# Feed-forward block of a recurrent decoder step: the RMS factor moved from the operands to the products, and the openings and closings of its parts reordered

## The chip, the cores and the metric

The kernel is one program on one core of a Trainium2 chip. Its metric is the device time of one execution, in microseconds (us). TensorE is written PE (PEld is its weight load), VectorE DVE, ScalarE ACT, GpSimd POOL, and SP issues the transfers.

## What is computed

Two layers of a hybrid decoder run on 576 tokens (512 of a prompt, 8 x 8 of samples), with activations kept as eight tiles `x[k]` of 128 channels x 576 tokens. Each layer is a recurrent mixer, a SwiGLU feed-forward and a gated per-layer embedding (ple). The change touches the feed-forward alone:

```
def _rmsnorm(x, g):
    y = xf * lax.rsqrt(jnp.mean(xf * xf, axis=-1, keepdims=True) + EPS)
    return (y * g.astype(F32)).astype(x.dtype)

def _swiglu(x, w1, w3, w2):
    return (jax.nn.silu(x @ w1) * (x @ w3)) @ w2

x = x + _swiglu(_rmsnorm(x, W['g_ffn'][i]), W['ffn_w1'][i], W['ffn_w3'][i], W['ffn_w2'][i])
```

The model width is 1024 and the hidden width 2816. The factor rsqrt(mean(x^2)+eps) is one number for each token, called `r` in the kernel.

## The kernel before

Every fp32 operand is split in a high and a low part (`whi`/`wlo` for weights, `bh`/`bl` for activations, `hh`/`hl` for hidden channels): ACT copies the high part to a rounded type, DVE subtracts it from the source. A product is then three matmuls, high x high, high x low, low x high. Weight tiles come by `wraw` (SP, two raw buffers) and are split by `wsplit`. Split weights live in two buffers of the pool `wp`, whatever they are for, so a new weight can be split only when PE is done with the one before the last.

`ffn` multiplies the 2x2 blocks of (w1, w3) with the 2x2 blocks of x (upper channels `x[0..3]` and lower `x[4..7]`, first and second half of the 576 tokens) by a seven-product scheme of the Strassen-Winograd kind. Its operands: `b11` and `b1` need the upper channels alone, `b21`, `b2`, `b3`, `b4`, `b22` the lower ones too. The eleven pairs of hidden tiles are run in three parts (`PARTS`: 4, 4 and 3 pairs). A pair is seven products of 24 matmuls, in this order: `head` (w13[p,0] by b11, into `mmx`), w13[p,1] by b21 (`mmy`), u by b2 (added on `mmx`), a22 by b1 (`mmz`), a21 by b3 (on `mmx`), the `head` of the next pair, w13[p,3] by b4 (on `mmx`), u by b22 (on `mmz`). Between them `mmx` is copied to SBUF by `copied` (line 1125) and the products are added up by `block`. After each part eight `gemm`s by w2 (line 210) are added to x by `add_out` (line 361). In the last pair of a part there is no head of a next pair between the third product on `mmx` and the fourth.

At the start of `ffn` the squares of `x[k]` are summed, `rnorm` makes `r` (PE sums over channels, DVE makes the inverse root in twelve small steps, PE broadcasts, ACT copies), and then DVE makes `g * x * r` (line 1092) and the differences (lines 1097 to 1103), which `operand` splits.

The program's text gives priorities. The order on each engine is fixed when the kernel is built, by a planner with its own estimates of durations: it takes the earliest instruction in the text that it believes ready, so a later one can go ahead of one that waits. The engines then run in that order. In layer 0 the embedding's products (`ple_up`) stand between the mixer and `ffn`; in layer 1 they are done inside the mixer, and the mixer's output projection, whose results POOL adds to x (line 359), comes right before.

Of the kernel before, what the change touches and what calls it, by code (L numbers as in the profile page):

```python
# [12 lines left out]
F = mybir.dt.float32  # L13
# [3 lines left out]
AF = mybir.ActivationFunctionType  # L17
# [31 lines left out]
OUT_V = ()  # L49
# [31 lines left out]
def trunk(ctx, tc, a, stop=None):  # L81
# [21 lines left out]
    def pcol(name, i=0, n=1):  # L103
        return par[:, PAR[name] + i:PAR[name] + i + n]
# [78 lines left out]
    def wload(ap, kt, eng=V):  # L183
        return wsplit(wraw(ap, kt), kt, wp, 2, eng=eng)
# [73 lines left out]
    def half(s):  # L258
        return slice(s * HF, (s + 1) * HF)
# [84 lines left out]
    def square_add(acc, src, first, eng=V):  # L344
        if first:
            S.activation(acc, src, AF.Square)
        else:
            sq = tmp("t2", 2)[:, :src.shape[-1]]
            one = S.activation(sq, src, AF.Square)
            two = eng.tensor_tensor(acc, acc, sq, op=OP.add)  # L350
            return one.ins, two.ins

    def add_out(m, ps, r=None):
        for s in range(2):
            xh, src = x[m][:, half(s)], ps[:, s]
            if r is not None:
                t = tmp("t1", 2)[:, :HF]
                V.tensor_tensor(t, src, r[:, half(s)], op=OP.mult)
                (V if m in OUT_V else G).tensor_tensor(xh, xh, t, op=OP.add)  # L359
            else:  # L360
                V.tensor_tensor(xh, src, xh, op=OP.add)  # L361

# [696 lines left out]
    def ffn(i, ha):  # L1059
        w13, w2 = a["w13"][i], a["w2"][i]  # L1060
        with tc.tile_pool(name=f"ffn{i}", bufs=1) as hp:
# [27 lines left out]
            (xg0, t0), (xg1, t1) = ([t_.bitcast(F) for t_ in hq()] for _ in range(2))  # L1089
            for xg, k0 in ((xg0, 0), (xg1, 4)):  # L1090
                for j in range(4):
                    V.scalar_tensor_tensor(xg[:, j], x[k0 + j], pcol("g_ffn", i * KD + k0 + j), r, op0=OP.mult, op1=OP.mult)  # L1092
                if k0 == 0:
                    b11 = operand(0, xg0[:, :, :HF])
            b21 = operand(1, xg1[:, :, :HF])
            d3, d2, d1, d4 = t0[:, :, :HF], t0[:, :, HF:], t1[:, :, :HF], t1[:, :, HF:]
            V.tensor_tensor(d3, xg1[:, :, HF:], xg0[:, :, HF:], op=OP.subtract)
            V.tensor_tensor(d2, d3, xg0[:, :, :HF], op=OP.add)
            b2 = operand(2, d2, -1.0)
            V.tensor_tensor(d1, xg0[:, :, :HF], xg0[:, :, HF:], op=OP.subtract)  # L1100
            b1 = operand(3, d1)
            b3 = operand(4, d3)
            V.tensor_tensor(d4, d2, xg1[:, :, :HF], op=OP.subtract)
            b4 = operand(5, d4)
            b22 = operand(6, xg1[:, :, HF:])

            def wsum(tag, src=None):
                t = hp.tile([P, 1024], F, tag=tag, name=tag, bufs=1)
                if src is not None:
                    nc.sync.dma_start(t, src)  # L1110
                return t
# [18 lines left out]
                prod([ps[:, n, :HF] for n in range(2)], wload(w13[p, 0], KD), b11, True)  # L1130
                return ps, copied(ps, "t1")

            def block(s, outs, dst, sign):
                for n in range(2):
                    V.tensor_tensor(s[:, n], s[:, n], outs[n], op=OP.add)
                S.activation(s[:, 0], s[:, 0], AF.Silu, scale=sign)
                if sign > 0:
                    V.tensor_tensor(dst, s[:, 0], s[:, 1], op=OP.mult)
                else:
                    V.scalar_tensor_tensor(dst, s[:, 1], sign, s[:, 0], op0=OP.mult, op1=OP.mult)  # L1140

            for p0, p1 in PARTS:
                hs = []
                for p in range(p0, p1):
# [6 lines left out]
                    ys = [bank("mmy")[:, :HF] for _ in range(2)]  # L1151
                    prod(ys, wload(w13[p, 1], KD), b21, True)
                    f1, f2 = tmp("rb", 2), tmp("t2", 2)
                    block(s1, ys, f1[:, :HF], 1.0)
                    a21, a22, a11, a12 = (wsum(f"a{n}", w13[p, n]) for n in (2, 3, 0, 1))
                    u = wsum("u")
                    V.tensor_tensor(a22, a22, a21, op=OP.add)
# [3 lines left out]
                    zs = [bank("mmz", "o")[:, :HF] for _ in range(2)]  # L1161
                    prod(zs, wsplit(a22, KD, wp, 2), b1, True)
# [3 lines left out]
                    block(s3, zs, f2[:, HF:], -1.0)  # L1166
# [8 lines left out]
                    block(s2, zs, f1[:, HF:], 1.0)  # L1175
# [283 lines left out]
```

## Time and profile before

| | us |
|---|---|
| median of three runs | 1871.07 (1869.39 to 1874.81) |
| the profiled execution | 1873.93 |
| its span in the trace | 1872.2 |

The trace is of the one profiled execution; 1.7 us of it lie outside the span. Times in rows count from the span's start. A matmul's duration in a row is modelled and overlaps the next, so PE is read by counts and starts: how many matmuls a stretch holds, and what they would need at the spacing of an undisturbed stretch.

### The profile page before, as it was taken

Reading aid. Unit: us, or ns where it says so; the run is one execution under the profiler, and the core shown is the slowest. Engines: PE = TensorE matmul, PEld = TensorE weight load, DVE = VectorE, ACT = ScalarE, POOL = GpSimd, SP = SyncE. Lnnn points to the kernel's source line nnn. Section 1 sums busy time; section 2 is a strip of 40 time slices with the busy share of each in tenths; the row PEclk is TensorE's granted clock in tenths of the full one; section 3 lists DMA queues with packets and bytes.
Section 4 is the critical chain, followed back from the end, with each engine's and each line's share of the span. In section 5 each row is a group of like instructions: output and inputs, shape, how many; then the busy total and the mean of one; then the engine's idle time right before and its main releaser. Section 6 shows DMA issues by size and latency. Waiting matters only on the chain. (4 is left out here: it accounts for less than half of the span.)

```text
span 1872.2 us, 32247 instructions
## 1 busy us (share of the span) xinstructions
PE 1748.0 (93%) x13134; PEld 1693.6 (90%) x13134; DVE 1343.1 (72%) x2256; ACT 811.7 (43%) x1341; POOL 415.1 (22%) x393
## 2 busy tenths in 40 slices
PE   7899989899999999989998999998959999999994
PEld 7789979899999999989987999998959999999994
DVE  6877784886377375588996897988587637737556
ACT  6654442554254143444553444535444325415332
POOL 2433343000000000033445537455510000000002
PEclk9999999899999999989998999999979999999997
DMA  5111113244244242312231322223315424424221
GB/s 191 57 62 66 68 49 130 83 160 139 91 162 154 87 147 71 118 41 72 103 111 68 109 104 85 96 100 108 118 52 167 133 86 168 147 91 144 71 80 51
DMA packets 63124, 193.74 MB, mean 103 GB/s; under 512 B 7040, under 2 KB 12800, under 8 KB 62976
## 3 DMA queue, kind: packets, MB, share of 16 engines
q1 hardware_dynamic: 62400, 191.10, 29.8%
q8 instruction: 103, 1.69, 0.4%
q10 hardware_dynamic: 576, 0.59, 0.1%
q14 instruction: 45, 0.37, 0.1%
HBM read 177.10 MB, written 14.56 MB: 102 GB/s over the span
## 5 line engine op out<-in xcount | busy, mean ns | idle before, releaser
L174 ACT ACTIVATE whi<-wraw 128x1024 fp32r<-128x1024 f32 (+2 forms) x213 | 221.5, 1040 | 392.6 <-PE mm L210 175.3
L175 DVE TENSOR_TENSOR wlo<-wraw,whi 128x1024 fp32r<-128x1024 f32 (+1 forms) x187 | 230.4, 1232 | 73.8 <-ACT whi L174 73.0
L1220 POOL TENSOR_TENSOR ev<-ev,rb 128x288 f32<-128x288 f32 x18 | 18.1, 1034 | 952.7 <-ACT rb L255 952.7
L1120 PE MATMUL mmx<-bh,whi 128*128 128x288 f32 x704 | 211.9, 301 | 14.8 <-ACT t L1125 9.3
L1120 PE MATMUL mmx<-bh,wlo 128*128 128x288 f32 x704 | 210.6, 299 | 4.8 <-DVE wlo L175 4.7
L1120 PE MATMUL mmx<-bl,whi 128*128 128x288 f32 x704 | 210.6, 299 | 2.9 <-DVE bl L163 2.9
L193 PE MATMUL mm<-xah,whi 128*128 128x288 f32 x632 | 191.4, 303 | 3.7 <-DVE hz L264 1.7
L193 PE MATMUL mm<-xal,whi 128*128 128x288 f32 x632 | 190.2, 301 | 0.0
L193 PE MATMUL mm<-xah,wlo 128*128 128x288 f32 x632 | 189.4, 300 | 0.0
L361 DVE TENSOR_TENSOR x<-mm,x 128x288 f32<-128x288 f32 x128 | 52.4, 451 | 169.1 <-PE mm L210 159.1
L193 PE MATMUL mm<-xch,whi 128*128 128x288 f32 x536 | 161.4, 301 | 2.9 <-DVE x L361 2.9
L193 PE MATMUL mm<-xch,wlo 128*128 128x288 f32 x536 | 160.8, 300 | 0.0
L193 PE MATMUL mm<-xcl,whi 128*128 128x288 f32 x536 | 160.7, 300 | 0.0
L210 PE MATMUL mm<-hl,whi 128*128 128x288 f32 x704 | 152.0, 296 | 0.0
L210 PE MATMUL mm<-hh,whi 128*128 128x288 f32 x704 | 151.7, 296 | 0.0
L210 PE MATMUL mm<-hh,wlo 128*128 128x288 f32 x704 | 151.3, 296 | 0.0
L1120 PEld LDWEIGHTS mmx<-bh,whi 128*128 128x128 f32 x704 | 134.5, 191 | 16.9 <-ACT t L1125 10.7
L1120 PEld LDWEIGHTS mmx<-bh,wlo 128*128 128x128 f32 x704 | 135.2, 192 | 6.6 <-DVE wlo L175 6.5
L1120 PEld LDWEIGHTS mmx<-bl,whi 128*128 128x128 f32 x704 | 134.9, 192 | 3.1 <-DVE bl L163 3.1
L193 PEld LDWEIGHTS mm<-xah,whi 128*128 128x128 f32 x632 | 120.0, 190 | 7.8 <-ACT lt L497 2.1
L193 PEld LDWEIGHTS mm<-xal,whi 128*128 128x128 f32 x632 | 120.2, 190 | 2.4 <-issue 1.8
L193 PEld LDWEIGHTS mm<-xah,wlo 128*128 128x128 f32 x632 | 120.1, 190 | 1.6 <-issue 0.9
(495 smaller groups left out, 4927.4 us busy)
## 6 DMA issues: line engine op xcount, KB each, us to landing
wraw<-w SPq DMA_DIRECT2D x98, 512.0 KB, 3.4
a<-w SPq DMA_DIRECT2D x88, 512.0 KB, 3.3
wraw<-w_sin SPq DMA_DIRECT2D x40, 512.0 KB, 3.3
wraw<-w_ein SPq DMA_DIRECT2D x22, 512.0 KB, 3.3
wraw<-wg SPq DMA_DIRECT2D x16, 512.0 KB, 3.2
s<-ss SPq DMA_DIRECT2D x16, 512.0 KB, 3.5
sss<-s SPq DMA_DIRECT2D x16, 512.0 KB, 2.8
wraw<-w_sout SPq DMA_DIRECT2D x16, 512.0 KB, 3.6
```

What stands on the lines that cost most here:

```text
L174: S.activation(hi, raw, AF.Copy)
L175: eng.tensor_tensor(lo, raw, hi.bitcast(F), op=OP.subtract)
L193: PE.matmul(ps, w[:, cols], v, start=(k == 0 and i == 0), stop=(k == n - 1 and i == 2))
L210: PE.matmul(ps[:, s, :HF], w[:, j * P:(j + 1) * P], m[:, half(s)], start=(k == 0 and i == 0), stop=(k == n - 1 and i == 2))
L361: V.tensor_tensor(xh, src, xh, op=OP.add)
L1120: PE.matmul(outs[n], w[:, o], v, start=(first and k == 0 and t_ == 0), stop=(k == 3 and t_ == 2), skip_group_check=not first)
L1220: eng.tensor_tensor(v, v, r[:, half(s)], op=OP.mult)
```

## The change

The operands become `g * x`, without `r`. `r` is multiplied into the first factor of each product of the hidden layer before its silu (one more DVE multiplication in `block` and one for the fourth product), and into the results of w2 in `add_out`, whose addition goes to DVE. The sums of squares and `rnorm` are moved behind the first operands. For the first pair, its head, the head of the second pair and its a22 product, all on the upper channels, stand ahead of everything that needs the lower channels, and the second pair's b21 product is moved into the first pair. In the last pair of a part half of the first w2 product (`next(dn)`, 24 matmuls) is placed ahead of the fourth product, and the last hidden tile's share of the first two w2 products goes to the end.

```diff
-    def add_out(m, ps, r=None):
+    def add_out(m, ps, r=None, eng=G):
...
-                (V if m in OUT_V else G).tensor_tensor(xh, xh, t, op=OP.add)
+                eng.tensor_tensor(xh, xh, t, op=OP.add)
...
-            for k in range(KD):
-                square_add(acc, x[k], k == 0)
-            rnorm([acc], D, 0, T, [(r, 1.0)])
...
-                    V.scalar_tensor_tensor(xg[:, j], x[k0 + j], pcol("g_ffn", i * KD + k0 + j), r, op0=OP.mult, op1=OP.mult)
...
+            def scaled(xg, k0):
+                for k in range(k0, k0 + 4):
+                    V.tensor_scalar(xg[:, k - k0], x[k], pcol("g_ffn", i * KD + k), None, op0=OP.mult)
+                    square_add(acc, x[k], k == 0)
+
+            scaled(xg0, 0)
+            b11 = operand(0, xg0[:, :, :HF])
             V.tensor_tensor(d1, xg0[:, :, :HF], xg0[:, :, HF:], op=OP.subtract)
+            b1 = operand(1, d1)
+
+            def lower():
+                scaled(xg1, 4)
+                bs = [operand(2, xg1[:, :, :HF])]
+                V.tensor_tensor(d3, xg1[:, :, HF:], xg0[:, :, HF:], op=OP.subtract)
+                V.tensor_tensor(d2, d3, xg0[:, :, :HF], op=OP.add)
+                bs.append(operand(3, d2, -1.0))
+                rnorm([acc], D, 0, T, [(r, 1.0)])
+                bs.append(operand(4, d3))
+                V.tensor_tensor(d4, d2, xg1[:, :, :HF], op=OP.subtract)
+                return bs + [operand(5, d4), operand(6, xg1[:, :, HF:])]
...
-            def block(s, outs, dst, sign):
+            def block(s, outs, dst, hf, sign):
                 for n in range(2):
                     V.tensor_tensor(s[:, n], s[:, n], outs[n], op=OP.add)
+                V.tensor_tensor(s[:, 0], s[:, 0], r[:, half(hf)], op=OP.mult)
                 S.activation(s[:, 0], s[:, 0], AF.Silu, scale=sign)
...
+            def down(p0, p1, hs):
+                def part(m, wts, ps, ks):
+                    for k in ks:
+                        h, l = hs[k]
+                        for t_, (w, v) in enumerate(((wts[0], h), (wts[0], l), (wts[1], h))):
+                            for s_ in range(2):
+                                PE.matmul(ps[:, s_, :HF], w[:, k * P:(k + 1) * P], v[:, half(s_)],
+                                          start=(k == 0 and t_ == 0), stop=(k == n - 1 and t_ == 2))
+
+                n = 2 * (p1 - p0)
+                got = []
+                for m in range(KD):
+                    wts = wload(w2[m][:, 2 * p0 * P:2 * p1 * P], n)
+                    ps = pm.tile([P, 2, 512], F, tag="mm", name="mm")
+                    got.append((m, wts, ps))
+                    if m == 0:
+                        part(*got[0], range(4))
+                        yield
+                        part(*got[0], range(4, n - 1))
+                    elif m == 1:
+                        part(*got[1], range(n - 1))
+                        for g in got:
+                            part(*g, [n - 1])
+                            add_out(g[0], g[2][:, :, :HF], r, V)
+                    else:
+                        part(*got[m], range(n))
+                        add_out(m, ps[:, :, :HF], r, V)
...
+                    if p == 0:
+                        nxt = head(1)
+                        wa = sums(0)
+                        zs = q5(wa[1])
+                        b21, b2, b3, b4, b22 = lower()
+                    ys = pre.pop("ys", None) or q2(p)
...
+                    if p:
+                        zs = q5(a22)
+                    else:
+                        pre["ys"] = q2(1)
...
-                    if p + 1 < p1:
+                    if p and p + 1 < p1:
                         nxt = head(p + 1)
+                    elif p:
+                        next(dn)
                     prod(xo, wload(w13[p, 3], KD), b4, False)
-                    S.activation(f2[:, :HF], xo[0], AF.Silu, scale=-1.0)
+                    V.tensor_tensor(f2[:, :HF], xo[0], r[:, :HF], op=OP.mult)
+                    S.activation(f2[:, :HF], f2[:, :HF], AF.Silu, scale=-1.0)
...
-                for m in range(KD):
-                    add_out(m, gemm(w2[m][:, 2 * p0 * P:2 * p1 * P], hs, False))
+                run(dn)
```

`q2` and `q5` are the b21 and the b1 products, `sums` loads the four blocks of a pair's weights and adds a21 to a22; each holds the lines that stood in the loop.

## Rows read from the trace of the kernel before

**Rows 1.** Profile page, part 1: busy us, share and instructions.

```profile
PE 1748.0 (93%) x13134; PEld 1693.6 (90%) x13134; DVE 1343.1 (72%) x2256; ACT 811.7 (43%) x1341; POOL 415.1 (22%) x393
```

**Rows 2.** Windows: stretch, its us, each engine's busy us (instructions), then PE clock.

```profile
456.00:491.00 35.00, 35.00 (x266) 35.00 (x265) 14.28 (x22) 7.96 (x9) 0.00 (x0) 1.00 0.31 95
352.80:376.00 23.20, 16.65 (x89) 15.38 (x88) 22.32 (x30) 14.86 (x25) 0.00 (x0) 0.78 0.19 68
1363.50:1412.00 48.50, 29.00 (x172) 27.32 (x171) 37.62 (x57) 21.24 (x30) 3.73 (x3) 0.75 0.16 55
1367.40:1391.20 23.80, 10.99 (x45) 10.42 (x46) 16.71 (x28) 6.53 (x8) 1.79 (x2) 0.50 0.07 22
```

**Rows 3.** Waits of PE, whole span: us in total, times, longest.

```profile
PE mmx L1120 <- ACT t L1125: 9.3, 6, 1.6
...
PE mmx L1120 <- DVE wlo L175: 4.7, 6, 1.6
```

**Rows 4.** Timeline, opening of layer 1's feed-forward: start us, us, engine, instruction.

```profile
1366.67 2.52 POOL L359 TENSOR_TENSOR x<-x,t 128x288 f32<-128x288 f32 x2 [1.95 <-DVE t L358]
...
1370.84 2.26 PE L233 MATMUL ssq<-cst,acc 128*128 128x1 f32 x10 [7.17 <-DVE acc L350]
...
1375.45 2.40 PE L252 MATMUL rbc<-cst,ry 128*128 128x128 f32 x10 [2.35 <-DVE ry L242]
...
1378.31 5.92 DVE L1092 SCALAR_TENSOR_TENSOR hh<-x,par,rb 128x576 f32<-128x576 f32 x8 [2.91 <-ACT rb L255]
...
1382.56 0.29 PEld L1120 LDWEIGHTS mmx<-bh,whi 128*128 128x128 f32 x1 [4.91 <-ACT bh L159]
```

**Rows 5.** Timeline of PE, opening of layer 0's feed-forward.

```profile
352.78 0.29 PE L193 MATMUL mm<-xah,wlo 128*128 128x288 f32 x1
353.35 0.40 PE L1120 MATMUL mmx<-bh,whi 128*128 128x288 f32 x1 [0.27 <-ACT bh L159]
356.06 0.54 PE L1120 MATMUL mmy<-bh,whi 128*128 128x288 f32 x2 [2.31 <-ACT bh L159]
```

**Rows 6.** Timeline of DVE in the same opening.

```profile
338.24 0.82 DVE L361 TENSOR_TENSOR x<-mm,x 128x288 f32<-128x288 f32 x2 [0.79 <-PE mm L193]
...
357.13 1.35 DVE L1097 TENSOR_TENSOR hl<-hh 128x1152 f32<-128x1152 f32 x1
```

**Rows 7.** One line each, DVE: us/1000 min/median/max, first and last start.

```profile
L541 DVE TENSOR_SCALAR ht<-hz x4: 447/454/459, 35.6 to 178.1; 128x576 f32<-128x576 f32 x4
L816 DVE TENSOR_SCALAR cu<-up,kp x24: 571/584/2431, 851.6 to 1272.2; 128x600 f32<-128x600 f32 x24
L350 DVE TENSOR_TENSOR acc<-acc,t x5: 745/752/759, 330.0 to 340.4; 128x576 f32<-128x576 f32 x5
L350 DVE TENSOR_TENSOR acc<-acc,t x7: 759/1211/1404, 1350.2 to 1369.9; 128x576 f32<-128x576 f32 x7
L1135 DVE TENSOR_TENSOR t<-t,mmz x88: 442/447/457, 383.9 to 1748.2; 128x288 f32<-128x288 f32 x88
L175 DVE TENSOR_TENSOR wlo<-u,whi x44: 1214/1226/1226, 366.2 to 1740.7; 128x1024 fp32r<-128x1024 f32 x44
```

**Rows 8.** Windows: the run-up to layer 0's and layer 1's feed-forward, steady pairs.

```profile
1344.00:1366.00 22.00, 19.40 (x144) 19.16 (x144) 13.40 (x20) 8.11 (x11) 17.53 (x16) 1.00 0.28 96
325.00:345.00 20.00, 17.51 (x133) 17.08 (x132) 14.92 (x26) 7.39 (x13) 0.98 (x1) 1.00 0.37 128
376.00:425.00 49.00, 49.00 (x370) 48.93 (x369) 38.63 (x48) 24.38 (x34) 0.00 (x0) 1.00 0.46 161
```

**Rows 9.** Timeline of ACT at the end of layer 0's first part.

```profile
442.20 1.06 ACT L174 ACTIVATE whi<-a 128x1024 fp32r<-128x1024 f32 x1 [1.23 <-PE mmx L1120]
...
448.52 1.06 ACT L174 ACTIVATE whi<-u 128x1024 fp32r<-128x1024 f32 x1 [2.14 <-PE mmx L1120]
449.48 0.63 ACT L1125 ACTIVATE t<-mmx 128x576 f32<-128x576 f32 x1
```

**Rows 10.** Timeline of PE at the same place.

```profile
448.32 0.29 PE L1120 MATMUL mmx<-bh,wlo 128*128 128x288 f32 x1
450.17 0.40 PE L1120 MATMUL mmx<-bh,whi 128*128 128x288 f32 x1 [1.55 <-ACT t L1125]
```

More of the change, by code (lines that the diff above doesn't have):

```diff
@@ L48 @@
 XRB = 1
-OUT_V = ()
 GT = [[4 * g, 4 * g + 1, 4 * g + 2, 4 * g + 3, 16 + g, 20 + g] for g in range(NG)]
@@ L1085, in ffn @@
             acc = tmp("acc", 1)
-            for k in range(KD):
-                square_add(acc, x[k], k == 0)
-            rnorm([acc], D, 0, T, [(r, 1.0)])
             (xg0, t0), (xg1, t1) = ([t_.bitcast(F) for t_ in hq()] for _ in range(2))
-            for xg, k0 in ((xg0, 0), (xg1, 4)):
-                for j in range(4):
-                    V.scalar_tensor_tensor(xg[:, j], x[k0 + j], pcol("g_ffn", i * KD + k0 + j), r, op0=OP.mult, op1=OP.mult)
-                if k0 == 0:
-                    b11 = operand(0, xg0[:, :, :HF])
-            b21 = operand(1, xg1[:, :, :HF])
-            d3, d2, d1, d4 = t0[:, :, :HF], t0[:, :, HF:], t1[:, :, :HF], t1[:, :, HF:]
-            V.tensor_tensor(d3, xg1[:, :, HF:], xg0[:, :, HF:], op=OP.subtract)
-            V.tensor_tensor(d2, d3, xg0[:, :, :HF], op=OP.add)
-            b2 = operand(2, d2, -1.0)
-            V.tensor_tensor(d1, xg0[:, :, :HF], xg0[:, :, HF:], op=OP.subtract)
[L1101 to L1105, printed above, removed]
+            d3, d2, d1, d4 = t0[:, :, :HF], t0[:, :, HF:], t1[:, :, :HF], t1[:, :, HF:]
+            def scaled(xg, k0):
[4 more added lines that the diff above has]
+            b11 = operand(0, xg0[:, :, :HF])
+            V.tensor_tensor(d1, xg0[:, :, :HF], xg0[:, :, HF:], op=OP.subtract)
+            b1 = operand(1, d1)
[9 more added lines that the diff above has]
+                return bs + [operand(5, d4), operand(6, xg1[:, :, HF:])]
             def wsum(tag, src=None):
@@ L1140, in block, with q2, sums, q5 @@
                     V.scalar_tensor_tensor(dst, s[:, 1], sign, s[:, 0], op0=OP.mult, op1=OP.mult)
+            def q2(p):
+                ys = [bank("mmy")[:, :HF] for _ in range(2)]
+                prod(ys, wload(w13[p, 1], KD), b21, True)
+                return ys
+            def sums(p):
+                a21, a22, a11, a12 = (wsum(f"a{n}", w13[p, n]) for n in (2, 3, 0, 1))
+                V.tensor_tensor(a22, a22, a21, op=OP.add)
+                return a21, a22, a11, a12
+            def q5(a22):
+                zs = [bank("mmz", "o")[:, :HF] for _ in range(2)]
+                prod(zs, wsplit(a22, KD, wp, 2), b1, True)
+                return zs
+            def down(p0, p1, hs):
[24 more added lines that the diff above has]
+                        add_out(m, ps[:, :, :HF], r, V)
+            pre = {}
             for p0, p1 in PARTS:
                 hs = []
+                dn = down(p0, p1, hs)
                 for p in range(p0, p1):
@@ L1150, in ffn @@
                     xo = [ps[:, n, :HF] for n in range(2)]
[L1151 to L1155, printed above, removed]
+                    if p == 0:
[4 more added lines that the diff above has]
+                    ys = pre.pop("ys", None) or q2(p)
+                    f1, f2 = hp.tile([P, T], F, tag="f1", name="f1", bufs=2), tmp("t2", 2)
+                    block(s1, ys, f1[:, :HF], 0, 1.0)
+                    if p:
+                        wa = sums(p)
+                    a21, a22, a11, a12 = wa
                     u = wsum("u")
-                    V.tensor_tensor(a22, a22, a21, op=OP.add)
                     V.tensor_tensor(u, a22, a11, op=OP.add)
@@ L1160, in ffn @@
                     s2 = copied(ps, "t2")
-                    zs = [bank("mmz", "o")[:, :HF] for _ in range(2)]
-                    prod(zs, wsplit(a22, KD, wp, 2), b1, True)
+                    if p:
+                        zs = q5(a22)
+                    else:
+                        pre["ys"] = q2(1)
                     V.tensor_tensor(a21, a21, a11, op=OP.add)
@@ L1165, in ffn @@
                     s3 = copied(ps, "t1")
-                    block(s3, zs, f2[:, HF:], -1.0)
-                    if p + 1 < p1:
+                    block(s3, zs, f2[:, HF:], 1, -1.0)
+                    if p and p + 1 < p1:
                         nxt = head(p + 1)
+                    elif p:
+                        next(dn)
                     prod(xo, wload(w13[p, 3], KD), b4, False)
-                    S.activation(f2[:, :HF], xo[0], AF.Silu, scale=-1.0)
+                    V.tensor_tensor(f2[:, :HF], xo[0], r[:, :HF], op=OP.mult)
+                    S.activation(f2[:, :HF], f2[:, :HF], AF.Silu, scale=-1.0)
                     V.scalar_tensor_tensor(f2[:, :HF], xo[1], -1.0, f2[:, :HF], op0=OP.mult, op1=OP.mult)
@@ L1174, in ffn @@
                     prod(zs, wsplit(u, KD, wp, 2), b22, False)
-                    block(s2, zs, f1[:, HF:], 1.0)
+                    block(s2, zs, f1[:, HF:], 1, 1.0)
                     split_to((hh[:, o], hl[:, o]), f1)
```

## The prediction

> **What bounds the kernel now.** The page's first part comes first: PE is busy for 93% of the span, DVE for 72% [rows 1], so the question is where PE stands still near the change. The windows answer it. In a stretch of w2 products PE starts 266 matmuls in 35.0 us, 0.1316 us each, at the full clock [rows 2]; that is the yardstick. Layer 0's opening, 23.2 us long, holds 89 matmuls, worth 11.7 us: 11.5 us are lost. Layer 1's opening, 48.5 us, holds 172 (20 of them the small ones of `rnorm`), worth 22.6 us: 25.9 us are lost [rows 2]. The table of waits adds the third place: the first matmul of the fourth product on `mmx` waited six times, 9.3 us in all, for the copy of `mmx` at line 1125 [rows 3]. Two layers by three parts make six, and the two timelines of a part's end show one of them: the last matmul of the third product starts at 448.32, ACT first splits a weight, then copies from 449.48 to 450.11, and PE goes on at 450.17 [rows 9, 10]. Start to start that is 1.85 us, 1.72 us more than a matmul needs; six cost 10.3 us. So 47.7 us lie where the change works.
>
> Why the openings cost what they do is read from the timelines. In layer 1 the last channel tile is added to x until 1369.19, the sums of squares reach PE at 1370.84, the scaling of the operands starts at 1378.31, and the first product at 1382.56 [rows 4]. PE has almost nothing to do from 1363.5 to there. In the stretch 1367.4 to 1391.2 its granted clock was 0.50, the 1.2 GHz level, and it had idled before that stretch and through most of it [rows 2]; so the first products ran at half speed too. Layer 0 has the embedding's products in front of the opening, so PE works until 352.78; then one matmul starts at 353.35 and the next at 356.06 [rows 5]. Its lower channels were complete at 339.06, and the first difference of operands is made at 357.13 [rows 6]: the factor and DVE lie in between.
>
> **Layer 0's opening.** Without the factor, DVE starts its chain at 339.06. It needs a scaling of x[7], 0.45 us, and a square's addition, 0.75 [rows 7]; three differences and the low parts of b21, b2 and b3 at 1.35 each [rows 6], 8.1 us; the low parts of b4 and b22 in eight pieces of 0.45, 3.6; `rnorm`'s small steps, 2.35 (1373.10, when PE's sums end, to 1375.45, when its broadcast starts [rows 4]); and the low parts of three weights, 3.7 at 1.23 [rows 7]. That makes 19 us, to 358. PE leaves the embedding at 352.8 and has three products on the upper channels, 72 matmuls or 9.5 us, before it asks for b21 at 362. Nothing is left to wait for but single weights, so 10.5 of the 11.5 us should go, with 6.5 as the lower bound (one operand late by 4 us, three entries of DVE's queue). Against it, DVE was busy 14.9 of 20 us in the run-up [rows 8] and gets eight scalings (3.6 us), one difference and two low parts (4.1) there or just behind; the mixer's results wait in PSUM for the same DVE. I charge 1 us (0 to 2). Gain 9.5.
>
> **Layer 1's opening.** x[1]'s square is added at 1350.2 and x[7]'s at 1369.9 [rows 7], so x[3] is complete near 1357 (an estimate, two of the six steps). b11 and b1 can then be split while PE still does the mixer's output, to 1363.5, and three products of 3.16 us keep it until 1373. b21 needs x[7] (1369.2), a scaling of 0.45 and ACT's copy of 1152 elements, 1.2 us by the 1.06 for 1024 [rows 9]: 1371 if DVE is free. It will not be quite free. From 1344 to 1366 DVE is busy 13.4 of 22 us with POOL at work for 17.5 [rows 8], and DVE's two-input additions beside POOL take 1.21 us in the median where they take 0.75 without it [rows 7]. New there are seven scalings, one difference and two low parts: 3.2 + 4.1 us at the undisturbed rows, which fits in the 8.6 us left; but at the disturbed ones, 7 x up to 2.43 (the longest of line 816) and 3 x 1.35 x 1.6, it is 23.5. x[7], b21 and the differences behind it then come later by some of the 15 us over. The Trainium skill, GPSIMD Engine Reference, section 1 (Specifications), says that GpSimd's SBUF interfaces are shared with VectorE and that VectorE instructions with two SBUF inputs, or in a mode with both ports, contend. These rows agree (1.21 us against 0.75); by that rule every new DVE instruction in the run-up would be slow, which is the third rival below.
>
> Behind x[7] DVE has the scaling, a square, low parts of b21 and b2, two differences (5.4), `rnorm`'s steps (2.35) and four weights' low parts (4.9) before the fifth product can run, 14 us from 1369.2, so to 1383; PE would have four products done by 1376.5. The small steps and one weight can come later, so I expect two waits of 2 to 3 us, some first matmuls that wait for a low part, and one stretch at the lower clock: 8 us lost in place of 25.9, and between 5 and 14. Gain 18 (12 to 21).
>
> **The ends of the parts.** The 24 matmuls put ahead of the fourth product are 3.2 us, more than the 1.85 of the copy: the 10.3 us go. But the first w2 weight now stays in one of the two split buffers from there until the last hidden tile is ready. The fourth product's weight, u, and the second w2 weight must pass through the other buffer one after another, and the third w2 weight waits for both. What a pass costs is in the rows: PE's last matmul of the buffer's old weight starts at 448.32 and takes its 0.13, ACT starts to split at 448.52 and takes 1.06, DVE's low part 1.23 [rows 7, 9, 10]. So 1.2 us to the first usable matmul, 2.4 to the low part. The fourth product's weight is covered by the 3.2 us. Behind it u is exposed; in a part of four pairs the w2 product's share of two finished hidden tiles, 12 matmuls or 1.6 us, can go in between if the planner puts it there, as it put two `mmy` matmuls into `mmx` in layer 0's opening [rows 5]; in the part of three pairs no finished tile is left. Then the second w2 weight: 6 matmuls (0.8 us) cover part of 1.2. Then the third: the other product's last 6 cover 0.8, and the output bank has to be read by two DVE multiplications first, with additions between, 1.35 us at 0.45 each [rows 7]. Lower bounds: 1.2 us for a four-pair part, 2.5 for a three-pair part. Upper, without interleaving and with the low part late each time: 3.5 and 5. I take 2.0 and 3.0, nearer to the lower since the planner does interleave: 4 x 2.0 + 2 x 3.0 = 14.0 in place of 10.3. Cost 3.7 (gain 0.5 to cost 13.7).
>
> **DVE in the pairs.** Each pair gets four multiplications of 288 columns, 0.45 us less some overlap, say 1.5 us; 22 pairs make 33 us of DVE. It is busy 38.6 of 49 us in steady pairs [rows 8], 17.4 of a pair's 22.1 (168 matmuls); then 18.9. Other work hides them as long as weights' low parts aren't late; those cost 4.7 us in six waits before [rows 3]. I charge 3 us (0 to 9). In the w2 stage DVE has 14.3 of 35 us [rows 2] and gets 8 x 0.9: hidden, since a product of 6.3 us lies between two uses of a bank. At the end of `ffn` the last x is 0.9 us later; the next stage's first products take the eight tiles in order, 24 matmuls, and reach the last one 2.8 us after their start: hidden.
>
> **The sum.** 9.5 + 18 - 3.7 - 3 = 20.8 us off the profiled 1873.9: 1853.1. The median of the three runs is 2.9 us under the profiled execution, so 1850 on the scale of the median, 1.1% less.
>
> **Rivals.** (1) Everything at its good bound: 11.5 + 21 + 0.5 = 33 us, 1838. For it, PE's 9.5 us of work on the upper channels; against it, DVE's load behind x[7]. Chance 0.18. (2) DVE becomes the bound of the pairs, half of its 33 us exposed in place of 3: 1864. For it, 18.9 of 22.1 us; against it, PE's few waits at 17.4. Chance 0.09. (3) The openings give half, because POOL slows the run-up, or because `rnorm` takes the PSUM banks that `mmy` needs until the factor is made: 13.7 in place of 27.5, so 1864. For it rows 7 and 8. Chance 0.15. (4) Slower: the single free split buffer. If at each part's end u and both w2 weights are fully exposed, 3 x 2.4 = 7.2 us, six ends cost 43 - 10.3 = 33; with 27.5 - 3 gained that is 8 us more, 1879. It decides from 5.8 us an end ((24.5 + 10.3) / 6). For it, ACT's splits already wait for PE [rows 9]; against it, the matmuls that can go in between. Chance 0.07. That the openings stay as they are would need b11 to be late as well; the rows show no reason, since the upper channels end well before PE does.
>
> **Chances.** My forecast, 1844 to 1858, has 0.51 (the rivals have 0.49). Changes under 0.3%, 5.6 us, are about what a measurement can't tell from none; rivals 2 and 3 straddle 1865.5 with their upper tails, so faster has 0.86, same 0.07, slower 0.07. The range 1837 to 1865 holds the forecast, most of rival 1 and the better half of rivals 2 and 3, 0.80 together; its ends are their bounds.
>
> **What would show it.** Right: no half-clock stretch of 20 us before layer 1's feed-forward; `mmx` and `mmz` matmuls right behind the mixer's; the six waits for line 1125 gone; new waits for `whi` of u and w2 at the parts' ends, 1 to 3 us each. Wrong: PE idle for over 4 us at 1363 or at 353; more than ten waits for low parts in the pairs; over 5 us at a part's end.

## The result, and the profile after

The changed kernel takes 1887.2 us (median), the kernel before 1874.5 in the same runs: ratio 1.0068, 95% interval 1.0047 to 1.0089. It is slower by 12.7 us, 9 to 17 by the interval, where 20.8 us less had been forecast. The profiled execution has a span of 1888.3 us (before 1872.2).

The page's first part shows the same work on PE and more on DVE; it answers to [rows 1]:

```profile
PE 1763.4 (93%) x13134; PEld 1699.4 (90%) x13134; DVE 1408.6 (75%) x2440; ACT 817.0 (43%) x1341; POOL 415.7 (22%) x393
```

Windows of the changed kernel (columns as in [rows 2]): layer 0's opening, layer 1's opening, and the end of layer 0's second part from the last matmul of the third product to the end of w2.

```profile
352.90:390.00 37.10, 35.38 (x260) 34.27 (x259) 28.94 (x52) 21.45 (x38) 0.00 (x0) 1.00 0.37 128
1372.10:1420.60 48.50, 36.01 (x208) 34.88 (x207) 38.45 (x61) 20.59 (x30) 4.58 (x4) 0.79 0.25 88
593.88:656.01 62.13, 59.06 (x434) 57.69 (x433) 31.34 (x53) 13.58 (x17) 0.00 (x0) 1.00 0.30 94
```

In layer 0's opening 260 matmuls now start in 37.1 us at the full clock, 2.9 us more than they need (260 x 0.1316 = 34.2). Layer 1's opening still has only 208 in 48.5 us, at a mean clock of 0.79. And the part's end takes 62.1 us for 434 matmuls, 5.0 more than the yardstick.

Where the time went is seen best by number: each execution starts 13134 matmuls on PE, and the start of the n-th can be set against the start of the n-th before. The table gives how much later or earlier (us) each stretch made the kernel, from the traces; the stretches are cut at matmuls 2032, 2530, 5203, 9553, 10060 and 12712, which start at 316.5, 396.8, 760.0, 1332.7, 1427.7 and 1788.2 us in the kernel before. The kernels are explained below.

| kernel | in front | opening, layer 0 | rest of its feed-forward | between | opening, layer 1 | rest of its feed-forward | behind | all |
|---|---|---|---|---|---|---|---|---|
| the change | 3.6 | -7.6 | 12.1 | -0.8 | -3.1 | 10.6 | 1.4 | 16.2 |
| ends_undone | 5.5 | -7.7 | 2.7 | -1.8 | -5.7 | 2.6 | -0.1 | -4.5 |
| interleave_alone | 2.3 | 0.2 | 6.0 | -1.1 | -0.6 | 8.4 | 0.3 | 15.6 |
| own_buffer | 5.4 | -7.7 | 6.8 | -2.6 | -5.7 | 6.8 | 0.7 | 3.6 |
| cover_held | 1.2 | -7.8 | 2.2 | -2.6 | -5.7 | 1.1 | 0.3 | -11.2 |
| factor_late | 4.1 | -3.1 | 9.2 | -2.6 | -10.3 | 10.7 | 0.3 | 8.4 |
| scale_on_act | 2.7 | -8.3 | 2.0 | -2.3 | -11.6 | 2.4 | 0.6 | -14.5 |
| scale_on_act_factor_late | 3.0 | -3.2 | 1.9 | 0.1 | -12.8 | 1.3 | 0.3 | -9.3 |
| order_undone | 0.6 | -7.6 | 1.7 | -1.4 | -7.0 | 2.8 | 1.2 | -9.7 |
| combined | 3.5 | -8.1 | 1.8 | -0.3 | -11.3 | 1.1 | 0.4 | -12.8 |
| old_order_held_cover | 1.7 | -5.5 | 1.3 | -0.4 | -7.8 | 1.1 | 0.1 | -9.4 |

What stands in front, between and behind is the same code in all of them; it scatters by some 5 us between single executions. The feed-forwards' columns are steadier, to some 3 us: layer 1's opening is the same code in the change, ends_undone, own_buffer and cover_held, and gains 3.1 in the first and 5.7 in the other three. The change gains 7.6 and 3.1 us in the openings (each with its run-up) and loses 12.1 and 10.6 behind them: 12.0 us, beside the 12.7 of the medians.

PE's waits in the whole span show the ends in one view (us in total, times, longest). In [rows 3] the copy of `mmx` had 9.3 us in six waits:

```profile
PE mmx L1122 <- DVE wlo L174: 6.2, 10, 1.3
PE mmz L1122 <- ACT whi L173: 6.1, 6, 1.0
...
PE mm L1166 <- DVE wlo L174: 5.6, 12, 0.6
...
PE mmx L1122 <- ACT t L1127: 3.2, 2, 1.6
...
PE mmz L1122 <- DVE wlo L174: 2.8, 6, 0.5
...
PE mm L1166 <- DVE t L357: 1.8, 6, 0.5
...
PE mm L1166 <- ACT whi L173: 1.1, 4, 0.3
```

The copy's six waits at the ends are gone, as forecast. In their place stand waits for u's weight (`mmz`, 6.1 + 2.8), for two w2 weights (`mm` L1166, 5.6 + 1.1) and for the bank that the scaled addition reads (1.8): 17.4 us for 9.3. And two waits for a copy are left, 3.2 us, that the forecast didn't have.

The timeline of PE at the end of layer 0's first part shows their order (only starts behind an idle time, and the rows around the end of the cover):

```profile
450.52 0.42 PE L1166 MATMUL mm<-hh,wlo 128*128 128x288 f32 x2
450.79 0.29 PE L1122 MATMUL mmx<-bh,wlo 128*128 128x288 f32 x1
...
454.89 0.40 PE L1122 MATMUL mmz<-bh,whi 128*128 128x288 f32 x1 [1.02 <-ACT whi L173]
456.15 0.40 PE L1122 MATMUL mmz<-bh,wlo 128*128 128x288 f32 x1 [0.47 <-DVE wlo L174]
461.67 0.53 PE L1166 MATMUL mm<-hh,whi 128*128 128x288 f32 x2 [0.27 <-ACT whi L173]
462.93 0.53 PE L1166 MATMUL mm<-hh,wlo 128*128 128x288 f32 x2 [0.47 <-DVE wlo L174]
470.06 0.51 PE L1166 MATMUL mm<-hh,whi 128*128 128x288 f32 x2 [0.21 <-DVE t L357]
471.47 0.53 PE L1166 MATMUL mm<-hh,wlo 128*128 128x288 f32 x2 [0.64 <-DVE wlo L174]
```

The w2 matmuls that could have stood in front of u are behind PE already: from 445.74 to 450.79 it starts 36 of them, the 24 for the copy and the 12 of the finished tiles. Nothing covers u at 454.89. Behind these two waits the granted clock is the lower one (1.2 GHz) for a while:

```profile
456.40:459.90 3.50, 3.50 (x16) 3.50 (x16) 2.78 (x5) 0.68 (x1) 0.00 (x0) 0.51 0.37 121
```

Sixteen matmuls take 3.5 us there, 1.4 more than at the yardstick. Only this end of the six shows it; nearly all of the loss at the ends is waiting, not the clock.

For layer 1's opening, PE's starts behind an idle time; they answer to [rows 4]:

```profile
1375.43 0.58 PE L1122 MATMUL mmx<-bh,whi 128*128 128x288 f32 x1 [3.11 <-issue]
1390.08 0.40 PE L1122 MATMUL mmx<-bh,whi 128*128 128x288 f32 x1 [1.12 <-ACT bh L161]
1393.55 0.61 PE L1122 MATMUL mmx<-bl,whi 128*128 128x288 f32 x1 [3.07 <-DVE bl L162]
1402.28 2.40 PE L251 MATMUL rbc<-cst,ry 128*128 128x128 f32 x10 [3.20 <-DVE ry L241]
1405.05 0.61 PE L1122 MATMUL mmy<-bh,whi 128*128 128x288 f32 x1 [0.37 <-ACT rb L254]
```

For the first wait, 3.11 us, the trace names no engine ("issue"). The head writes into a bank of the pool that holds the mixer's results, and DVE ends its reading of the last but one of these at 1375.34, 0.09 us before PE starts:

```profile
1374.89 0.45 DVE L357 TENSOR_TENSOR t<-mm,rb 128x288 f32<-128x288 f32 x1
```

In ends_undone, own_buffer, cover_held, factor_late and factor_early this distance is 0.10 or 0.11 us, so the wait is very likely for that bank: DVE has the low part of b1 in its queue between the two halves of the reading.

DVE's timeline in the same stretch, from the first to the last of the factor's small steps:

```profile
1389.60 0.15 DVE L235 TENSOR_SCALAR ms<-ssq 128x5 f32<-128x5 f32 x1
1389.68 1.21 DVE L174 TENSOR_TENSOR wlo<-u,whi 128x1024 fp32r<-128x1024 f32 x1
1390.81 1.35 DVE L1106 TENSOR_TENSOR hl<-hl,hh 128x1152 f32<-128x1152 f32 x1
...
1392.15 1.35 DVE L162 SCALAR_TENSOR_TENSOR bl<-hl,bh 128x1152 fp32r<-128x1152 f32 x1
...
1395.90 1.55 DVE L159 TENSOR_TENSOR bl<-hl,bh 128x288 fp32r<-128x288 f32 x4
1397.37 1.55 DVE L159 TENSOR_TENSOR bl<-hh,bh 128x288 fp32r<-128x288 f32 x4
...
1402.06 0.17 DVE L241 SCALAR_TENSOR_TENSOR ry<-rt,ry 128x5 f32<-128x5 f32 x1
```

The chain that took 2.35 us before [rows 4] lasts from 1389.60 to 1402.23, because DVE has other operands' work between its steps. DVE waits for another engine once there, for 0.65 us.

### The profile page after: what moved, and what is told of

It is laid out like the page before. It is cut to its first block, busy times and chain, and to the rows that moved or that the text cites. A ratio compares the mean times of both kernels' runs of the same rounds, so it can differ in the third digit from the quotient of the medians.

```text
span 1888.3 us, 32465 instructions
## 1 busy us (share of the span) xinstructions
PE 1763.4 (93%) x13134; PEld 1699.4 (90%) x13134; DVE 1408.6 (75%) x2440; ACT 817.0 (43%) x1341; POOL 415.7 (22%) x393
## 5 line engine op out<-in xcount | busy, mean ns | idle before, releaser
L357 DVE TENSOR_TENSOR t<-mm,rb 128x288 f32<-128x288 f32 x160 | 66.5, 451 | 137.7 <-PE mm L1166 120.4
L1166 PE MATMUL mm<-hh,wlo 128*128 128x288 f32 x704 | 152.4, 297 | 5.6 <-DVE wlo L174 5.6
L1166 PE MATMUL mm<-hh,whi 128*128 128x288 f32 x704 | 151.9, 297 | 3.0 <-DVE t L357 1.8
L1166 PE MATMUL mm<-hl,whi 128*128 128x288 f32 x704 | 151.2, 296 | 0.0
```

What stands on the lines that cost most here:

```text
L1166: PE.matmul(ps[:, s_, :HF], w[:, k * P:(k + 1) * P], v[:, half(s_)], start=(k == 0 and t_ == 0), stop=(k == n - 1 and t_ == 2))
```

## The experiments

All kernels are the changed one with the edit shown, unless said otherwise. Ratios are to the kernel before, with 95% intervals. The letters in the expectations: **A**, the ends of the parts make the kernel slower, because the cover is spent early and a split buffer is held; **D**, layer 1's opening waits for VectorE's sum of work; **F**, it waits for the factor's chain and its banks; **C**, VectorE is slowed beside GpSimd; **O**, the new order costs what it gives. The changed opening or VectorE's added work as the cause of the loss is the rival to A. The expectations of the first four kernels use some letters otherwise: B in them is the rival to A; C in own_buffer is a wrong place of the cover; in factor_late, D is what is F here, and E is C.

**ends_undone.** The old w2 loop, with the factor in its additions:

```diff
-                    elif p:
-                        next(dn)
...
-                run(dn)
+                for m in range(KD):
+                    add_out(m, gemm(w2[m][:, 2 * p0 * P:2 * p1 * P], hs, False), r, V)
```

> The changed kernel with the ends of its parts put back: no w2 matmuls ahead of the fourth product, eight whole w2 products after the pairs (r still multiplied into their results on VectorE). Theory A (the first w2 weight, held in one of two split buffers, makes the next weights wait; 4.6 us lost at an end of four pairs, 4.1 at one of three, in place of 1.7): six ends go back to 1.7 us, 16 us less than the changed kernel, ratio to the kernel before about 0.998. Rival B (the multiplications by r on VectorE cost it): those stay, so within 4 us of the changed kernel, ratio 1.005 to 1.007.

Measured: 1866.5 us, 0.9965 (0.9953 to 0.9978). So the ends cost 1.0068 / 0.9965, 1.0% or 19 us, and the rest of the change is a gain. The copy's waits are back, now eight: six at the ends and one for each layer's first pair. Waits of PE:

```profile
PE mmx L1122 <- ACT t L1127: 12.5, 8, 1.6
```

Windows of this kernel: the end of layer 0's second part, and layer 1's opening.

```profile
591.55:651.05 59.50, 57.95 (x435) 57.71 (x434) 30.92 (x53) 13.59 (x17) 0.00 (x0) 1.00 0.32 98
1363.00:1411.50 48.50, 36.00 (x224) 34.93 (x223) 39.88 (x63) 21.68 (x32) 4.60 (x4) 0.82 0.27 89
```

The old end takes 59.5 us for 435 matmuls, 2.3 over the yardstick; the changed one 5.0. In the table the rest of the two feed-forwards costs 5.3 us with the old ends and 22.7 with the changed ones: 17.4 for six ends, 1.4 of it the stretch at the lower clock above.

**interleave_alone.** The kernel before with `down` and the `next(dn)` of the change, and no factor on the products.

> The kernel before with only the part ends of the change (w2 matmuls ahead of the fourth product, last hidden tile's share at the end); no r in the products, old opening. Theory A: 4.6 and 4.1 us lost at an end in place of 1.7, so 14 to 17 us slower than before, ratio 1.008. Rival B: the interleaving by itself gains up to 10 us, ratio 0.995 to 1.000.

Measured: 1888.4 us, 1.0079 (1.0055 to 1.0104), 15 us slower by itself. The same waits stand in its table:

```profile
PE mmz L1120 <- ACT whi L174: 7.9, 8, 1.0
...
PE mmz L1120 <- DVE wlo L175: 2.8, 6, 0.5
```

In the table it loses 14.4 us behind the openings. A holds from both sides, and DVE's added work isn't needed for it.

**own_buffer.** The first four tiles' part of the first w2 weight gets split buffers of its own (512 columns); the rest of it is loaded after the `yield`. To make room, `f1` shares the buffers of `rb` and `acc`:

```diff
-                    wts = wload(w2[m][:, 2 * p0 * P:2 * p1 * P], n)
+                    if m:
+                        wts = wload(w2[m][:, 2 * p0 * P:2 * p1 * P], n)
+                    else:
+                        wts = [wsplit(wraw(w2[0][:, 2 * p0 * P:2 * p0 * P + SEQ], 4), 4, hp, 1, SEQ)]
...
                         yield
+                        wts.append(wload(w2[0][:, 2 * p0 * P + SEQ:2 * p1 * P], n - 4))
```

> The changed kernel, but the first four tiles of the first w2 weight have split buffers of their own (the two tiles f1 are taken from buffers that lie idle, to make room). Theory A: the weight of u finds a free buffer while the fourth product runs, so the 2.05 us of lost time in that product go at all six ends, and the second w2 weight no longer waits; 12 to 18 us less than the changed kernel, ratio about 0.999. Rival B (VectorE): nothing changes, ratio 1.005 to 1.008. Rival C (the planner put the covering matmuls in the wrong place): lost time in u's product stays over 1.5 us.

Measured: 1876.3 us, 1.0006 (0.9992 to 1.0019). The waits for u's weight are gone and 11 us with them, but the copy's eight waits are back:

```profile
PE mmx L1122 <- ACT t L1127: 12.6, 8, 1.6
```

With its weight there early, the cover was issued early: in layer 0's first part its 24 matmuls start between 437.85 and 444.70, among earlier products of the same pair; the third product on `mmx`, whose copy they were to cover, starts only at 447.35. So the held buffer is one half of A, the place of the cover the other.

**cover_held.** own_buffer, with the 24 covering matmuls tied behind the last matmul of the third product:

```diff
-                    prod(xo, wsplit(a21, KD, wp, 2), b3, False)
+                    end[0] = prod(xo, wsplit(a21, KD, wp, 2), b3, False)
...
-                        part(*got[0], range(4))
+                        with after_all(end[0]):
+                            part(*got[0], range(4))
```

> As own_buffer (1876.3 us), and the 24 matmuls of w2 that are to cover the wait for the copy are tied behind the last matmul of the third product, so that they cannot be issued earlier. Theory A (the cover was spent early): the six waits of 1.9 us for the copy go, less what the last of the 24 adds, and the time falls by 10 to 12 us, to 1864 to 1866. Rival: the 24 matmuls only move a wait on, since the fourth product's own weights or u's then come late: 1870 to 1876.

Measured: 1864.9 us, 0.9963 (0.9949 to 0.9977): less than own_buffer by 11.4 us in the medians, by 8 in the ratios (the two were measured beside different runs of the kernel before) and by 10.3 behind the openings in the table, from nothing but the order of PE's queue. Two waits for the copy are left (the first pairs), and the second part's end loses 58.86 - 434 x 0.1316 = 1.7 us:

```profile
PE mm L1168 <- DVE wlo L174: 3.3, 6, 0.6
PE mmx L1122 <- ACT t L1128: 3.2, 2, 1.6
```

```profile
587.33:646.19 58.86, 58.01 (x434) 57.57 (x433) 30.12 (x53) 13.39 (x17) 0.00 (x0) 1.00 0.33 99
```

The old end was at 2.3. The interleave, mended, is worth 2.0 us over all ends (3.3 against 5.3 in the table), too little for the times to show (0.9963 against 0.9965): a w2 weight still passes late, 3.3 us of waits.

**factor_late.** In the changed kernel, `rnorm` is called behind the additions of the first block:

```diff
-                rnorm([acc], D, 0, T, [(r, 1.0)])
...
+                if "r" not in pre:
+                    pre["r"] = rnorm([acc], D, 0, T, [(r, 1.0)])
                 V.tensor_tensor(s[:, 0], s[:, 0], r[:, half(hf)], op=OP.mult)
```

> The changed kernel with the factor's computation moved behind the additions of the first b21 product, so that its PSUM banks are asked for after those of that product. Theory D (in layer 1's opening the b21 products wait for the factor's banks: 3.4 us before the broadcast, 0.7 before the first b21 matmul, and a low clock after): 4 to 7 us less than the changed kernel, all in layer 1's first pair, ratio 1.003 to 1.005. Rival E (VectorE beside GpSimd in the run-up is all of it): within 2 us of the changed kernel.

Measured: 1883.5 us, 1.0054 (1.0034 to 1.0073); its interval overlaps that of the changed kernel. By the table layer 1's opening gains 10.3 us in place of 3.1 (5.7 in the three other kernels with that opening), and layer 0's 3.1 in place of 7.6: in layer 0 the first pair has two waits for the copy (1.56 and 0.59 us) for one (1.61), and its clock is 0.50 from 378.3 to 381.7; in layer 1 the 3.2 us before the broadcast are gone. What is left there, beside the first wait of 3.1, are mainly waits for DVE's low parts; the two longest:

```profile
1388.44 0.40 PE L1121 MATMUL mmy<-bh,wlo 128*128 128x288 f32 x1 [1.39 <-DVE wlo L174]
...
1400.54 0.61 PE L1121 MATMUL mmx<-bh,wlo 128*128 128x288 f32 x1 [2.96 <-DVE wlo L174]
```

**factor_early.** ends_undone, with `rnorm` called right after the last square instead:

```diff
                 scaled(xg1, 4)
+                rnorm([acc], D, 0, T, [(r, 1.0)])
                 bs = [operand(2, xg1[:, :, :HF])]
...
-                rnorm([acc], D, 0, T, [(r, 1.0)])
```

> As ends_undone, with the factor computed as soon as the last square is added, ahead of the operands of the lower channels. Theory F: the chain of the factor's small steps ends some 6 us earlier (it was spread from 1379.4 to 1391.2 among steps of 1.2 to 1.5 us), the broadcast's wait of 3.4 us goes, and the time is 1862 to 1864. Theory D: the small steps only change places with the operands' low parts, for which TensorE then waits as long: 1865 to 1868.

Measured: 1864.2 us, 0.9955 (0.9934 to 0.9976), not to be told from ends_undone. It tells little: the planner put the chain's steps where they were, and the waits are those of ends_undone to 0.2 us (3.09 for the low part, 3.21 for the broadcast).

**scale_on_act.** ends_undone, with the scalings on ScalarE:

```diff
-                    V.tensor_scalar(xg[:, k - k0], x[k], pcol("g_ffn", i * KD + k), None, op0=OP.mult)
+                    S.activation(xg[:, k - k0], x[k], AF.Copy, scale=pcol("g_ffn", i * KD + k))
```

> The changed kernel with the old part ends (as ends_undone, 1866.5 us), and with the eight scalings of each layer's opening on ScalarE in place of VectorE. Theory D: in layer 1's opening everything waits for VectorE, which was busy 27.9 of the 32 us from 1363 to 1395 in ends_undone while ScalarE was busy 15.6. The eight scalings took 0.5 to 0.9 us each there, some 5 us in all; VectorE gets through that stretch 4 to 6 us sooner and the time is 1861 to 1863. Rival, theory F: the opening waits for the factor's chain of small steps and for its PSUM banks, whose length does not hang on VectorE's load: 1865 to 1867. Should ScalarE become late instead, its whole-stage copies come later and the time is above 1868.

Measured: 1859.2 us, 0.9935 (0.9914 to 0.9956), the lowest of all kernels here, 0.65% under the kernel before. The window of layer 1's opening:

```profile
1357.30:1405.80 48.50, 38.98 (x259) 36.84 (x258) 42.87 (x68) 25.92 (x39) 5.67 (x4) 0.89 0.30 98
```

In 48.5 us 259 matmuls start, where ends_undone had 224. The opening's gain grows from 5.7 to 11.6 us, layer 0's hardly changes. Of these 5.9 us up to 3.4 are the clock, 0.89 in place of 0.82 over 48.5 us. The text of the factor's chain was not touched, so F alone doesn't explain it; D does.

**scale_on_act_factor_late.** Both edits on ends_undone.

> As scale_on_act, and the call that computes the factor is moved behind the first additions that need it, as in factor_late. Theory D alone: the factor's place gives nothing once VectorE has less to do, 1861 to 1864, the same as scale_on_act. Theory F: the wait of 3.4 us before the broadcast goes, and with it 3 us, 1862 to 1864 while scale_on_act stays at 1866. Both at once: 1858 to 1860.

Measured: 1863.9 us, 0.9955 (0.9938 to 0.9973): nothing on top of scale_on_act. Layer 1's opening gains 12.8 us in its trace (scale_on_act 11.6), layer 0's 3.2 (8.3). The two edits mend the same stretch, so they don't add up; that taking the small steps out of DVE's queue, or the scalings, lets the same operands come sooner is argued, not shown.

**adds_on_vector.** ends_undone, with the last group's 16 additions of the odd mixer on VectorE:

```diff
-            add_out(m, ps, r)
+            add_out(m, ps, r, eng)
...
+                run(mix_out(..., V if q.g == NG - 1 else G))
```

> As ends_undone (1866.5 us), with the additions of the last group of the odd mixer's output on VectorE in place of GpSimd. Theory C: in the run-up to layer 1's opening VectorE loses 6 to 10 us of busy time because its additions and scalings take up to 2.9 us beside GpSimd's additions and 0.5 to 0.75 us otherwise; the 16 additions cost VectorE some 7 us at 0.44 us each, and the time is 1862 to 1867. Rival, theory D alone (VectorE is loaded, whoever else runs): 7 us more of work on the engine that sets the end of that stretch, 1871 to 1875.

Measured: 1865.1 us, 0.9961 (0.9946 to 0.9976), the same as ends_undone with 16 more instructions on DVE. The squares' additions there, by line (as in [rows 7]):

```profile
L349 DVE TENSOR_TENSOR acc<-acc,t x7: 746/751/759, 1344.7 to 1370.4; 128x576 f32<-128x576 f32 x7
```

and in the changed kernel, with the scalings:

```profile
L349 DVE TENSOR_TENSOR acc<-acc,t x7: 746/1352/2942, 1358.0 to 1384.0; 128x576 f32<-128x576 f32 x7
L1090 DVE TENSOR_SCALAR hh<-x,par x8: 511/792/2266, 1353.3 to 1383.6; 128x576 f32<-128x576 f32 x8
```

C is right that GpSimd slows DVE here: 2.9 us against 0.76 at the longest. The Trainium skill, SBUF — State Buffer, section "Who interferes with whom", says that an instruction of VectorE with two SBUF inputs contends with a GpSimd instruction that reads SBUF, and that a scaling can, in a mode with two ports; both lines agree. But taking the additions from GpSimd for the price that they have on DVE is an even trade: the time is inside C's range and outside D's.

**order_undone.** Old ends and the old order of the opening: squares, factor, scalings, all operands of the lower channels, `head(1)` and the second and fifth products at their old places. What is left of the change is the factor on the products.

> The old part ends and the old order of the opening (squares, factor, scalings, operands of the upper channels after all of them, head, second and fifth product in their old places): what is left of the change is that the factor multiplies the products. If the opening's gain comes from taking the factor off the operands' path alone, the scalings no longer wait for it and the time is near ends_undone, 1865 to 1868. If it comes from the new order of the channels and products, 1874 to 1877, with VectorE's added multiplications as a small loss. I take a part of each, 1870.

Measured: 1863.9 us, 0.9956 (0.9940 to 0.9973). I had taken a part of each cause; with the scalings on DVE the order of channels and products gives nothing that shows. PE's two longest waits in layer 1's opening:

```profile
1368.88 2.26 PE L232 MATMUL ssq<-cst,acc 128*128 128x1 f32 x10 [6.63 <-DVE acc L349]
...
1377.60 0.61 PE L1120 MATMUL mmx<-bl,whi 128*128 128x288 f32 x1 [5.75 <-DVE bl L162]
```

and its window:

```profile
1357.00:1405.50 48.50, 34.07 (x226) 32.70 (x225) 41.31 (x65) 24.25 (x35) 4.79 (x4) 0.82 0.27 93
```

Two long waits for DVE in place of four of 1 to 3 us, 226 matmuls in the window against 224, and 7.6 and 7.0 us gained in the openings, as against 7.7 and 5.7.

**combined.** cover_held with the scalings on ScalarE, and 18 matmuls of cover in place of 24.

> The changed kernel with the scalings on ScalarE (scale_on_act) and with held, own-buffered cover at the part ends (cover_held), of which only 18 matmuls are held for the copy and six more are left for the wait behind u's product. By the parts: cover_held stood at 0.9963 of before, scale_on_act took 0.003 off ends_undone, and six matmuls of 0.13 us more behind u should take some 0.8 us off what each of six ends still loses in w2, 1.94 to 2.28 us: 1854 to 1858, ratio 0.990 to 0.992. If the scalings help only because they fill a different gap than the ends leave, or 18 matmuls don't last through the copy, 1859 to 1862.

Measured: 1861.3 us, 0.9938 (0.9926 to 0.9950). The forecast was too good: the six matmuls taken out of the tie were issued early all the same, and the ends lost what they lose in cover_held (2.9 us behind the openings in its trace, 3.3 there). With the ends worth only 2 us, the two edits together can't be told from scale_on_act alone.

**old_order_held_cover.** order_undone with cover_held's ends and the scalings on ScalarE.

> The old order of the opening (order_undone, 1863.9 us), with the scalings on ScalarE (scale_on_act) and the held cover at the part ends (cover_held): of the change, the factor on the products and a mended interleave are left. Theory D: the order of the channels gives nothing, VectorE's work in the opening does, so this stands where combined stands (0.9938), 1858 to 1862, ratio 0.992 to 0.995. Rival, theory O: the new order costs what it gives, since it leaves the first pair's last copy uncovered (1.9 us in each layer), and with VectorE relieved the old order is better by 3 us or more: 1853 to 1858, ratio 0.989 to 0.9915. Should the new order be what gains once VectorE has room: 1864 and above.

Measured: 1862.6 us, 0.9943 (0.9928 to 0.9958), not to be told from combined. D's range of ratios held, O's didn't. The traces say more than the times: with the scalings on ScalarE in both, the openings gain 5.5 and 7.8 us in the old order, and 8.1 and 11.3 in the new (combined). So in the old order the scalings' move is worth next to nothing (7.6 and 7.0 in order_undone), and the new order is ahead once DVE has less to do; one trace of each, and medians 1.4 us apart, don't prove it.

## Why the prediction was wrong, step by step

**The ends of the parts** are the step that turned the sign. The forecast knew the mechanism (rival 4: one free split buffer, u and two w2 weights passing through it in turn) and sized it wrongly: 3.7 us with 13.7 as the upper bound. Measured, it costs 15 us by itself (interleave_alone) and 19 within the change (ends_undone; 17.4 in the table). Two readings failed. First, "if the planner puts it there": 12 matmuls were to stay in front of u, and the planner put them beside the cover of the copy, where 24 were enough; u is bare in every part, 6.1 + 2.8 us. Secondly, the third w2 weight: 0.8 us of cover was thought to meet most of it; together with the second one, `mm` waits 8.5 us at six ends. By the table an end takes (17.4 + 10.3) / 6 = 4.6 us, the copy's 1.72 no longer in it, where the forecast had 2.0 and 3.0. By PE's starts an end of four pairs takes 4.5 us, or 6.0 where the clock fell, past its upper bound of 3.5, and one of three pairs 4.0, below its 5.

Rival 4's turning point, 5.8 us an end, was worked out with openings that gain 24.5 us after DVE's 3. They gained 10.7 in the table and the pairs cost 5.3, so it lay at (5.4 + 10.3) / 6 = 2.6, and 4.6 is past it.

**Layer 1's opening** was forecast at a gain of 18, with 12 as the lower bound, and gave 3.1 in the profiled execution and 5.7 in three others of the same code; 1.5 of that difference is the clock, 0.79 and 0.82 over 48.5 us. First, PE was to go on from the mixer's output to three products on the upper channels without a pause; it ran them, but 3.1 us later, behind the bank above. The step that failed most is "14 us from 1369.2, so to 1383": it left out work that DVE takes up before PE can go on. The last addition to x ended at 1380.56 (the sum of the row below), 4 us later than forecast (the stretch begins 7.3 us late, by the table), and the chain at 1402.23, 21.7 us behind it. In between stand, beside the terms I had, the difference d4, the low part of b3 (1.35 each), u's sum (1.21) and the low parts of the last operands (1.55 twice), 7.0 us. Also, the small steps did not come "later" as one piece: each waits for the one before, and between the first four DVE put 2.3 to 3.6 us of other work, in pieces of 1.2 to 1.6. Of the third rival, which had this opening give half, the first reason (POOL slows the run-up) is seen in L349 and L1090; the second (banks) is seen at 1402.28 to 1405.05, where the broadcast comes before `mmy`. That DVE's queue sets the stretch is borne out by scale_on_act (the eight scalings, 7.7 us of DVE in ends_undone, off it; 5.9 us more gained there), by factor_late (the chain out of the queue, 4.6 more than 5.7) and by order_undone (another order of the same work, nothing lost). Against it as the only cause stand adds_on_vector and old_order_held_cover.

POOL's last additions to x in the changed kernel:

```profile
1378.79 1.77 POOL L358 TENSOR_TENSOR x<-x,t 128x288 f32<-128x288 f32 x2 [2.20 <-DVE t L357]
```

**Layer 0's opening**: the number is right, 7.6 for 9.5, with 1.6 of the difference in the copy below; the reason only in part, since order_undone says that the factor off the operands' path brings it, not the channels' order. Up to 5.1 of the 11.5 us lost there before were the clock (0.22 of 23.2 us [rows 2]).

**Missed altogether**: the first pair. `head(1)` and the fifth product were moved into the opening, and they had covered the two copies of that pair. `q2(1)` took one place; the other copy is bare in each layer, 1.61 us of waiting, as PE's timeline shows:

```profile
1418.17 0.40 PE L1122 MATMUL mmx<-bh,whi 128*128 128x288 f32 x1 [1.61 <-ACT t L1127]
```

**DVE in the pairs**: 5.3 us (the rest of both feed-forwards in ends_undone) for 3, within its bounds. The waits of `mmx` on low parts went from 4.7 us in six [rows 3] to 6.2 in ten; rival 2 is out.

In sum: 7.6 + 3.1 - 17.4 - 5.3 = -12.0 us, where the forecast had 9.5 + 18 - 3.7 - 3 = 20.8. The two terms that failed are 15 and 14 us off, to the same side. What stays open is how the 5.9 us and the 4.6 us of the two remedies in layer 1's opening overlap in detail, why the scalings' move gave so little in the old order, and why factor_early moved nothing: the order in which the planner gives DVE its work was seen, not varied by itself.

## What to carry to other kernels

Work that is to cover a wait has to be tied to it: an issue order made by a planner spends it wherever it fits first, and here the tie alone was worth 8 to 11 us. Before a weight is loaded early, count what must pass through the other buffers while it is held; and before a product is moved forward, look for the wait that it had covered. Where one engine's sum of work sets a stretch, a new order by itself only exchanged waits here (order_undone); taking work off that engine paid (scale_on_act), though by the traces in the new order alone. Add up all of that engine's queue, not only what stands on the path in the source.

## What the runs showed of the hardware

Short stretches at the lower clock behind gaps of some 3 us. In layer 1's opening of the changed kernel the windows show three of them at 1.2 GHz, each beginning near the end of a wait or inside it; before there was one of 23.8 us [rows 2]:

```profile
1374.60:1381.50 6.90, 6.07 (x25) 6.10 (x26) 6.58 (x9) 0.86 (x2) 3.76 (x4) 0.51 0.32 118
1391.70:1398.50 6.80, 4.95 (x20) 4.95 (x21) 6.80 (x14) 2.77 (x8) 0.00 (x0) 0.50 0.29 108
1401.90:1408.80 6.90, 6.15 (x26) 5.96 (x26) 0.75 (x3) 1.99 (x3) 0.00 (x0) 0.51 0.23 76
```

In the first, PE had stood for 3.1 us and then worked without a pause; 25 matmuls took 6.07 us from 1375.43, 2.8 more than at the full clock. So the wait of 3.1 us there cost about twice its length. That price isn't fixed: in ends_undone a wait of 3.10 us at the same place was followed by half as long a stretch at the lower clock:

```profile
1366.50:1369.90 3.40, 3.40 (x16) 3.40 (x16) 3.40 (x6) 0.68 (x1) 1.20 (x2) 0.50 0.00 0
1369.90:1373.30 3.40, 3.40 (x27) 3.40 (x26) 3.20 (x3) 2.17 (x3) 1.49 (x2) 1.00 0.46 157
```
